# The first mixer's x takes shift and scale in one step, and three context projections and the context's gate products stand ahead of it

## The chip, the cores and the metric

The kernel runs on one core of a Trainium2 chip. The metric is the device time of one execution in microseconds. A run here is such an execution, and the time before is the median of three. One further execution was recorded by the profiler, and all rows below come from that one.

## The reference

The program computes two blocks, one after the other, on 256 tokens of width 1024. The first step, the one that is changed here, is a gated DeltaNet mixer over a latent stream x and a context stream of 256 tokens each:

```
sh1, sc1, ... = split(silu(c) @ ada_w + ada_b, 6)          # for the context: silu(c_ctx)
h  = rms_norm(x) * norm_mix * (1 + sc1) + sh1              # modulate; hl for x, hc for the context
qkv, z, gates, pool_in = split(h @ w_in)
qkv = silu(dw_conv(qkv, conv_w))                           # width 3, along the tokens, zero padded
beta = sigmoid(gates[:2]);  log_decay = -exp(a_log) * softplus(gates[2:] + dt_bias)
o   = gated delta rule over chunks of 64 (k, v of both streams; q of x), forwards and backwards
y   = [rms_norm(o) * silu(z), pooled(pool_in)] @ w_out;    x = x + g1 * y
```

A mixture of 16 experts follows, then a second layer with a short convolution and again 16 experts, and then the second block (an RG-LRU/SSD layer and a stick-breaking layer). None of these is touched by the change.

## The kernel before

**Layout.** Activations lie transposed: 128 features on the partitions, 8 slices of features (`kt`), 256 tokens in a row. Each product runs in three fp32r matmuls per slice, since both weight and activation are split into a high part and a low part (`ws`, lines 344 to 346: high by high, high by low, low by high). The high part is a copy on ScalarE (`wh`, `hl`, `hc`, line 213) and the low part a subtraction on VectorE (`wl`, line 299). `hl` holds x's two parts, `hc` the context's.

**Shift and scale.** The first 8 MB of ada weights (8 tiles) give scale (`ada_first(0)`) and then shift (`ada_first(1)`) of both streams as columns: matmuls at line 482, a copy `adar`, four transposes `adaT`, a reduction and an addition into `adac` (x) and `adax` (context). `norm_in` (line 516) makes `hc` and `hl` from the scale alone. The shift enters later, in two ways. For the projections whose result goes through the convolution, columns 256 and 257 of `hl` hold the two shift columns, so one matmul gives both the projected tokens and the projected shift. The convolution adds the projected shift as a bias, and `edges` (line 691) takes off what that bias must not give at the first and last token (line 555). For the rest, `whole` (unit `U`, line 934) adds the shift to all 8 slices of `hl` and splits them again: on VectorE `lat` and the low part, on ScalarE the high part.

**The hand-written order.** `ORDER["mixer0"]` is a string of units, issued one after another; a scheduler then places the instructions on each engine. kN and vN are the context's projection of head N (`project_ctx`, into `qkvc`); KN, VN and QN are x's projection (`qkv`), with convolution and activation; G is the gates (`qd`: the gate products of x, then of the context; `cum`: sums of the log decays); W0 and W1 are the decay matrices (GpSimd's affine_select and the matmuls `DT`); RN is `correlate` (`kk`), with which a head's matrix A is made; D is `diagonal`, 31 dependent steps on VectorE between L763 and L774; I0 and I1 finish the inverse (`lv`); P0 to P3 run the chunks; Z is the projection of z and of the pooling input (`zp`), which reads the whole `hl`; A0 to A4 are the other ada products, 8 tiles of 1 MB each and 40 in all, at line 439; C0 and C1 are the scores. After the mixer come its output projection (`res`) and the first experts.

**The queue of loads.** SyncE issues all large loads in program order (line 261): the first ada tiles, the mixer's weights (`ev_ws`), the 40 ada tiles through two buffers, `ev_ts`, `ev_out`, and then the experts' `wg`, `wu` and `wd`. A load waits until its buffer is free and holds back all loads behind it.

Of the kernel before, what the change touches and what calls it, by code (L numbers as in the profile page):

```python
# [13 lines left out]
P = 128  # L14
D = 1024
# [8 lines left out]
WARM = 5, 10  # L24
ADA_SUM = ()
# [152 lines left out]
class Kernel:  # L178
# [180 lines left out]
    def quad(self, pool, w32, rhs, n, toks, shift=None):  # L359

        nc = self.nc
        a = self.ps("qd", "a")
        for kt in range(KT):
            q = kt % 4
            r = rhs(kt)
            for i, x in enumerate(r):
                nc.tensor.matmul(a[32 * q:32 * q + 32, :x.shape[1]], w32(kt), x, start=(kt < 4 and i == 0),
                                 stop=(kt >= 4 and i == len(r) - 1), tile_position=(0, 32 * q))  # L370
        s = pool.tile([P, 512], F32, tag="quad", name="quad", bufs=1) if pool else self.work("hid", "quad", 512)
        if shift is None:
            self.copy(s[:, :n], a[:, :n], "act")
        else:
            t, i = shift
            m = t.shape[1]
            if x.shape[1] > n:
                nc.vector.tensor_copy(t, a[:, n:n + m])
            nc.scalar.activation(s[:, :n], a[:, :n], AF.Identity, bias=t[:, i:i + 1])
# [94 lines left out]
    def ada_first(self, i, pool):  # L474
# [12 lines left out]
        for t in range(4):  # L487
            self.tp(b[:, t * P:(t + 1) * P], r[:, t * P:(t + 1) * P])
# [21 lines left out]
    def norm_in(self, pool, wk, hs):  # L510
# [19 lines left out]
        tags = iter(("a", "a", "a", "ps") * 2)  # L530
        for s, f in ((1, s_c), (0, s_l)):
            for ft in range(0, KT, 2):
# [4 lines left out]
                for j in range(2):  # L537
                    self.split_scaled(a[:, 256 * j:256 * j + 256], f[:, ft + j:ft + j + 1],
                                      *(t[:, ft + j, :256] for t in hs[s]))

    def conv3(self, out, a, wc, edges=None):


        for i, x in enumerate(a):
            o = out[:, 256 * i:256 * i + 256]
            if edges is None:
                self.nc.scalar.activation(o, x, AF.Copy, scale=wc[1])
            else:
                self.nc.scalar.activation(o, x, AF.Identity, scale=wc[1], bias=edges[:, i, 2:3])
            self.stt(o[:, 1:], x[:, :255], wc[0], o[:, 1:], OP.mult, OP.add)  # L550
            self.stt(o[:, :255], x[:, 1:], wc[2], o[:, :255], OP.mult, OP.add)
        if edges is not None:
            n = len(a)
            e3 = out[:, :256 * n].rearrange("p (s t) -> p s t", s=n)[:, :, ::255]
            self.nc.vector.tensor_sub(e3, e3, edges[:, :n, :2])
# [12 lines left out]
    def mixer0(self, xin, xp):  # L568
# [20 lines left out]
        self.ada_first(1, xin)  # L589
# [6 lines left out]
        for j, x in enumerate((self.adac[0], self.adax)):  # L596
            self.split(x[:, 0:8], *(t[:, :, 256 + j] for t in hs[0]), "dve")
# [15 lines left out]

        def gates():

            gt = pr.tile([P, 4, 16], F32, name="gates")
            gb = pr.tile([P, 2], F32, name="gate_shift")
            ew = lambda kt: self.col("evgate", 32 * kt, 32)
            for s in range(2):
                gp = self.quad(wk, ew, lambda kt: [t.bitcast(F32) for t in (lat, ctx)[s](kt)], 256, [(0, P), (P, P)], (gb, s))  # L620
# [9 lines left out]
            cum = self.ps("cum", "b")  # L630
# [11 lines left out]
        for dr in range(2):  # L642
            v.tensor_copy(m_out[dr], (self.m_gt, self.m_lt)[dr])

        def decays(dr):
# [3 lines left out]
                                                    base=0, channel_multiplier=-sg)  # L649
            for tt in range(4):  # L650
# [21 lines left out]

        def project_ctx(part, h):

            a = self.ps("qkvc", "b")[:, :256]
            self.ws(a, "ev_ws", 4 * part + h, ctx)
            first[part, h] = a

        def project(part, h):
# [4 lines left out]
            self.ws(a[:, :258], "ev_ws", 4 * part + h, lat)  # L684
# [5 lines left out]
            edges = wk.tile([P, 2, 3], F32, tag="edges", name="edges", bufs=2)  # L690
            v.tensor_mul(edges, a[:, 256:258].unsqueeze(2).to_broadcast([P, 2, 3]), dne[:, i:i + 1].to_broadcast([P, 2, 3]))
# [250 lines left out]
        units = {"G": gates, "W0": each(decays(0), 4), "W1": each(decays(1), 4), "U": whole, "D": invert, "C0": lambda: scores(0), "C1": lambda: scores(1), "Z": each(zpool(), 4)}  # L942
# [69 lines left out]
    def warm(self, n):  # L1012

        x = self.xT.rearrange("p k t -> p (k t)")
        a = self.ps("warm", "ada")
        for i in range(n):
            self.nc.tensor.matmul(a[:, :256], self.ident, x[:, :256], start=True, stop=True)
# [963 lines left out]
```

## Time and profile before

| | us |
|---|---|
| runs | 1247.2, 1247.69, 1238.82 |
| median of the runs | 1247.2 |
| profiled execution, its own time | 1233.16 |
| its span (first to last instruction) | 1231.4 |
| busy: TensorE (PE) / VectorE (DVE) / ScalarE (ACT) / GpSimd (POOL) | 1087.1 / 627.6 / 482.3 / 64.5 |
| first projection of x starts (K0) | 46.44 |
| D starts, on VectorE | 113.82 |
| the inverse starts (`lv`, PE) | 176.18 |
| output projection starts (`res`, PE) | 265.84 |
| first `wd` load issued | 303.95 |

PE is the busiest engine (88% of the span), but the shares are means over stages with different limits; the stages of the mixer are read one by one below. From 320 to 520 us the DMA engines are full (share 1.01, 421 GB/s) while PE is busy for 154.89 of 200 us. A row of the timeline gives its start, its duration, engine, line, operation, result<-inputs and the number of instructions, and in brackets the engine's idle time before it and what ended that. A row of the windows gives the stretch, its length, the busy time of PE, PEld (weight loads into PE), DVE, ACT and POOL with the number of instructions in parentheses, then the granted clock of TensorE (1.00 is the upper level, 2.4 GHz), the busy share of the DMA engines and what they moved in GB/s.

### The profile page before, as it was taken

How to read it: one execution, taken by the hardware profiler on the slowest of the kernel's cores; microseconds unless marked ns; L12 is line 12 of the kernel's file. 1: busy time of each engine (PE TensorE's matmuls, PEld its weight loads, DVE VectorE, ACT ScalarE, POOL GpSimd, SP SyncE). 2: the span in 40 equal slices, each digit the busy share in tenths (PEclk: the TensorE clock that was granted, in tenths of full speed). 3: DMA queues.
4: the chain of work that ended last, by engine and by line, in shares of the span. 5: the costliest groups of instructions: out<-in, count | busy, mean ns of one | idle time of the engine just before them, and what ended most of it. 6: DMA issues, size and time to landing. Idle time of an engine off the chain costs nothing.

```text
span 1231.4 us, 19493 instructions
## 1 busy us (share of the span) xinstructions
PE 1087.1 (88%) x7788; PEld 743.5 (60%) x7788; DVE 627.6 (51%) x1422; ACT 482.3 (39%) x995; POOL 64.5 (5%) x112
## 2 busy tenths in 40 slices
PE   5899889989997666899999766669999999999997
PEld 2667756678443020499863312028897789988875
DVE  3548973363312010478431101028787888689875
ACT  4347543243101000455420100016777566566663
POOL 0050000000000000000000000000001100011100
PEclk9899989989999686999999977789999999999999
DMA  9568567878999999997479999993352145432220
GB/s 384 236 231 305 208 262 240 296 274 367 419 421 420 422 422 422 421 420 290 169 277 421 423 422 420 421 421 111 136 205 82 56 172 189 171 136 106 104 103 35
DMA packets 48042, 339.71 MB, mean 276 GB/s; under 512 B 5328, under 2 KB 5584, under 8 KB 7248
## 3 DMA queue, kind: packets, MB, share of 16 engines
q1 hardware_dynamic: 46800, 336.38, 69.2%
q10 hardware_dynamic: 1152, 2.09, 0.5%
q8 instruction: 61, 1.00, 0.3%
q14 instruction: 29, 0.24, 0.1%
HBM read 337.40 MB, written 1.05 MB: 275 GB/s over the span
## 4 chain that ended last, share of the span: by engine, by line
PE 53%; DMA 27%; DVE 8%; issue 7%; ACT 3%; POOL 2%; POOLq 0%; SPq 0%; DVEq 0%; ACTq 0%
DMA w<-wu 10%; DMA w<-wd 8%; DMA w<-wg 6%; PE ada L439 3%; PE gu L1178 3%; PE sc L346 2%; PE sc L345 2%; PE sc L344 2%; DMA pk<-pk 2%; PE qkvg L344 2%; PE qkvg L346 2%; PE qkvg L345 2%; DVE wl L299 1%; PE res L345 1%; PE res L344 1%
## 5 line engine op out<-in xcount | busy, mean ns | idle before, releaser
L213 ACT ACTIVATE wh<-w 128x512 fp32r<-128x512 f32 x304 | 188.3, 629 | 149.6 <-PE res L345 27.3
L299 DVE TENSOR_TENSOR wl<-w,wh 128x512 fp32r<-128x512 f32 x304 | 208.1, 694 | 74.4 <-ACT wh L213 68.5
L1178 PE MATMUL gu<-w,xg 128*32 128x512 f32 x1024 | 161.0, 734 | 49.6 <-DMA w<-wu 24.8
L1178 PEld LDWEIGHTS gu<-w,xg 128*32 128x32 f32 x1024 | 26.9, 118 | 168.7 <-DMA w<-wu 75.3
L1204 PE MATMUL dn<-w,hidT 128*32 128x512 f32 x512 | 69.3, 638 | 24.9 <-DMA w<-wd 19.1
L1193 DVE TENSOR_TENSOR hid<-hid,gu 128x512 f32<-128x512 f32 x8 | 5.5, 685 | 162.0 <-PE gu L1178 162.0
L213 ACT ACTIVATE y<-dn 128x512 f32<-128x512 f32 x16 | 9.6, 597 | 188.6 <-PE dn L1204 188.6
L234 DVE SCALAR_TENSOR_TENSOR xT<-sc,adac,xT 128x256 f32<-128x256 f32 x64 | 27.9, 479 | 105.4 <-PE sc L1212 105.4
L344 PE MATMUL qkvg<-u_f,wh 128*128 128x272 f32 (+1 forms) x256 | 74.4, 291 | 0.0
L346 PE MATMUL qkvg<-u_f,wl 128*128 128x272 f32 (+1 forms) x256 | 73.2, 286 | 0.0
L345 PE MATMUL qkvg<-u_f,wh 128*128 128x272 f32 (+1 forms) x256 | 72.8, 284 | 0.0
L1204 PEld LDWEIGHTS dn<-w,hidT 128*32 128x32 f32 x512 | 13.9, 113 | 68.9 <-DMA w<-wd 41.1
L346 PE MATMUL sc<-hT,wl 128*128 128x258 f32 x192 | 54.5, 284 | 0.9 <-DVE wl L299 0.9
L344 PE MATMUL sc<-hT,wh 128*128 128x258 f32 x192 | 54.7, 285 | 0.2 <-DVE xT L234 0.2
L345 PE MATMUL sc<-hT,wh 128*128 128x258 f32 x192 | 54.3, 283 | 0.0
L344 PEld LDWEIGHTS qkvg<-u_f,wh 128*128 128x128 f32 x256 | 48.1, 188 | 3.2 <-issue 2.0
L346 PEld LDWEIGHTS qkvg<-u_f,wl 128*128 128x128 f32 x256 | 48.3, 189 | 0.8 <-issue 0.8
L345 PEld LDWEIGHTS qkvg<-u_f,wh 128*128 128x128 f32 x256 | 48.2, 188 | 0.0
L439 PE MATMUL ada<-w,cs 128*32 128x512 f32 x320 | 46.4, 630 | 0.0
L1192 ACT ACTIVATE hid<-gu 128x512 f32<-128x512 f32 x8 | 4.8, 597 | 103.5 <-PE gu L1178 103.5
L1212 PE MATMUL sc<-sg,y 128*128 128x256 f32 x128 | 35.6, 427 | 8.4 <-ACT y L213 8.4
L1212 PEld LDWEIGHTS sc<-sg,y 128*128 128x128 f32 x128 | 25.4, 208 | 25.8 <-ACT y L213 22.5
(606 smaller groups left out, 2620.3 us busy)
## 6 DMA issues: line engine op xcount, KB each, us to landing
w<-wu SPq DMA_DIRECT2D x64, 1024.0 KB, 19.8
w<-wg SPq DMA_DIRECT2D x64, 1024.0 KB, 19.8
w<-wd SPq DMA_DIRECT2D x64, 1024.0 KB, 19.8
w<-ada SPq DMA_DIRECT2D x48, 1024.0 KB, 5.7
w<-f_in SPq DMA_DIRECT2D x16, 1024.0 KB, 4.8
w<-sc_in SPq DMA_DIRECT2D x12, 1024.0 KB, 19.8
w<-e_out SPq DMA_DIRECT2D x8, 1024.0 KB, 4.8
w<-ev_ws SPq DMA_DIRECT2D x6, 1024.0 KB, 5.9
```

Source lines behind the costliest of these rows:

```text
L213: return self.nc.scalar.activation(out, in_, AF.Copy)
L234: return self.nc.vector.scalar_tensor_tensor(out, a, s, b, op0=op0, op1=op1, **kw)
L299: self.nc.vector.tensor_sub(lo, x, hi.bitcast(F32))
L344: mm(out, wh, xh, start=(kt == 0), stop=False)
L345: mm(out, wh, xl, start=False, stop=False)
L346: self.last_mm = mm(out, wl, xh, start=False, stop=(kt == nk - 1)).ins
L439: nc.tensor.matmul(a[32 * q:32 * q + 32, :], self.cs[:, kt, :], w[:, q * 512:(q + 1) * 512], start=(kt == 0), stop=(kt == KT - 1), tile_po ...
L1178: nc.tensor.matmul(a[32 * e:32 * e + 32, :], xg[g // 2][:, kt, s:s + 32], w[:, e * 512:(e + 1) * 512], start=(kt == 0), stop=(kt == KT - 1 ...
L1192: nc.scalar.activation(hid, pu[0], AF.Silu)
L1193: v.tensor_mul(hid, hid, pu[1])
L1204: nc.tensor.matmul(a[32 * e:32 * e + 32, :], hT[:, t, 32 * e:32 * e + 32], w[:, e * 512:(e + 1) * 512], start=(t == 0), stop=(t == 3), til ...
L1212: nc.tensor.matmul(a[:, j * 256:(j + 1) * 256], y[:, (2 * f2 + j) * P:(2 * f2 + j + 1) * P], sg[g // 2][:, g % 2], start=True, stop=True)
```

## The change

x's slices are made after the shift is known, by one step that scales and shifts (`affine`, in turn on ScalarE and VectorE) into `lat`, and are then split. `ada_first(1)` moves into `norm_in`, behind the context's slices. Unit U is gone. Columns 256 and 257 of `hl` now hold the context's shift alone, and the edges are kept for the context's half of K and V only; Q has none and is 256 columns wide. The gate products are a function of their own, `gates_of`: the context's become unit g. Twelve matmuls on constants (`warm`) are added behind the first `adaT`. In the order, k1, k0, g and k2 stand ahead of K0; A tiles, W steps, Q3 and the pieces of Z move as well. Two heads of a context projection share one PSUM bank, and the later context projections and the gate products of the context are held until the shift's last matmul is issued.

```diff
-    "mixer0": "k0 G W1 K0 W1 W0 W0 A0 W1 W0 W1 W0 k1 K1 k2 K2 A1 k3 K3 Q0 R0 R1 R2 R3 v0 V0 v1 V1 v3 V3 v2 V2 Q1 Q2 "
-              "Q3 D A2 I0 I1 A3 I0 I0 I0 U P0 P0 I1 A4 P1 Z I1 I1 C1 C0 P1 Z P2 Z Z P2 P3 P3",
+    "mixer0": "k1 k0 g G k2 K0 W1 W1 W0 A0 W0 W0 W1 W0 K1 K2 A1 k3 W1 K3 Q0 R0 R1 R2 R3 v0 V0 v1 V1 v3 V3 v2 Q3 V2 "
+              "Q1 Q2 D A2 I0 I1 I0 I0 A3 I0 P0 Z P0 I1 A4 Z P1 I1 I1 C1 C0 P1 P2 Z P2 Z P3 P3",
...
+        if i == 0:
+            with self.tc.issue_after(pe.ins):
+                self.warm(WARM0, "b", self.ones)
...
-        for s, f in ((1, s_c), (0, s_l)):
+        for s in (1, 0):
...
+                for k in (ft, ft + 1):
+                    x = a[:, 256 * (k - ft):][:, :256]
+                    if s:
+                        self.split_scaled(x, s_c[:, k:k + 1], *(t[:, k] for t in hs[s]))
+                    else:
+                        t = wk.tile([P, 256], F32, tag="lat", name="lat", bufs=2)
+                        self.affine(t, x, s_l[:, k:k + 1], self.adac[0][:, k:k + 1])
+                        self.split(t, *(t[:, k, :256] for t in hs[s]))
+            if s:
+                self.ada_first(1, pool)
...
-        self.ada_first(1, xin)
+        shift = self.first_mm
...
+        def gates_of(s):
+            with tc.issue_after(shift) if s else ExitStack():
+                qd[s] = self.quad_products(ew, lambda kt: [t.bitcast(F32) for t in (lat, ctx)[s](kt)])
...
         def project_ctx(part, h):
-            a = self.ps("qkvc", "b")[:, :256]
-            self.ws(a, "ev_ws", 4 * part + h, ctx)
+            if (part, h // 2) not in banks:
+                banks[part, h // 2] = self.ps("qkvc", "b")
+            a = banks[part, h // 2][:, 256 * (h % 2):][:, :256]
+            with tc.issue_after(shift) if first else ExitStack():
+                self.ws(a, "ev_ws", 4 * part + h, ctx)
...
-            edges = wk.tile([P, 2, 3], F32, tag="edges", name="edges", bufs=2)
-            v.tensor_mul(edges, a[:, 256:258].unsqueeze(2).to_broadcast([P, 2, 3]), dne[:, i:i + 1].to_broadcast([P, 2, 3]))
+            edges = None
+            if part < 2:
+                edges = wk.tile([P, 3], F32, tag="edges", name="edges", bufs=2)
+                v.tensor_scalar(edges, dne[:, i], a[:, 256:257], None, op0=OP.mult)
...
-        def whole():
-            for ft in range(KT):
-                t = wk.tile([P, 256], F32, tag="sq", name="lat")
-                hi, lo = (t[:, :256] for t in lat(ft))
-                self.stt(t, hi.bitcast(F32), self.adac[0][:, ft:ft + 1], lo.bitcast(F32), OP.add, OP.add)
-                self.split(t, hi, lo)
```

On PE, from the last tiles of the first ada weights to K0, the order before was as follows (`ada` with the waits on DMAHW6 and DMAHW7 are the last two tiles; `qkv` begins K0):

```order
L346 MATMUL qkvc<-hc_292,wl 128x256
L482 MATMUL ada<-w,cs 32x512 [waits DMAHW6_49]
...
L482 MATMUL ada<-w,cs 32x512 [waits DMAHW7_49]
...
L206 MATMUL adaT<-ident,adar 128x128 [waits Activation_49]
...
L369 MATMUL qd<-hl_290,pkg 32x258 [waits DVE_49]
L369 MATMUL qd<-hl_291,pkg 32x258 [waits DVE_49]
...
L344 MATMUL qkv<-hl_290,wh 128x258
```

The same place now:

```order
L486 MATMUL ada<-w,cs 32x512 [waits DMAHW6_49]
...
L486 MATMUL ada<-w,cs 32x512 [waits DMAHW7_49]
...
L207 MATMUL adaT<-ident,adar 128x128 [waits Activation_49]
...
L347 MATMUL qkvc<-hc_305,wl 128x256
L372 MATMUL qd<-hc_305,pkg 32x256
...
L372 MATMUL qd<-hl_303,pkg 32x258 [waits DVE_49,Activation_49]
L372 MATMUL qd<-hl_304,pkg 32x258 [waits DVE_49]
...
L345 MATMUL qkv<-hl_303,wh 128x258
```

The first context projection (k1) now ends ahead of the last two ada tiles; k0, the context's gate products and k2 stand behind them, and x's gate products are spread through k2. Before, only k0 stood ahead, and the context's gate products came after K0 had begun.

On VectorE, in the second half of D, the order before (`sub` and `ident` are D's steps, `wl` a weight's low part, `lat` and `hl` unit U):

```order
L770 TENSOR_TENSOR sub<-B,ident_465 128x112 [waits DVE_49]
L234 SCALAR_TENSOR_TENSOR lat<-hl_290,adac_103,hl_291 128x256 [waits DVE_49]
L771 TENSOR_TENSOR ident_465<-ident_465,sub 128x4x28 [waits DVE_49]
L299 TENSOR_TENSOR wl<-w,wh 128x512 [waits Activation_49]
L770 TENSOR_TENSOR sub<-B,ident_465 128x87 [waits DVE_49]
L299 TENSOR_TENSOR hl_291<-lat,hl_290 128x256 [waits Activation_49]
L771 TENSOR_TENSOR ident_465<-ident_465,sub 128x3x29 [waits DVE_49]
```

The same place now:

```order
L799 TENSOR_TENSOR sub<-B,ident_492 128x112 [waits DVE_49]
L800 TENSOR_TENSOR ident_492<-ident_492,sub 128x4x28 [waits DVE_49]
L799 TENSOR_TENSOR sub<-B,ident_492 128x87 [waits DVE_49]
L800 TENSOR_TENSOR ident_492<-ident_492,sub 128x3x29 [waits DVE_49]
L799 TENSOR_TENSOR sub<-B,ident_492 128x60 [waits DVE_49]
```

The sixteen instructions of U are gone from between D's steps, and the weights' parts stand further ahead.

On SyncE, at the end of the mixer, the loads before:

```order
L261 DMA w<-ada 128x2048 [waits DMAHW7_49,PE_49]
L261 DMA w<-wu 128x2048 [waits DMAHW1_49,PE_49]
L261 DMA w<-wu 128x2048 [waits DMAHW2_49,PE_49]
L261 DMA w<-ev_out 128x2048 [waits DVE_49,Activation_49]
L261 DMA w<-wg 128x2048 [waits DVE_49,PE_49,DMAHW0_49,Activation_49,Pool_49]
```

The same place now:

```order
L262 DMA w<-ada 128x2048 [waits DMAHW7_49,PE_49]
L262 DMA w<-ada 128x2048 [waits DMAHW0_49,PE_49]
L262 DMA w<-ev_out 128x2048 [waits DVE_49]
L262 DMA w<-wg 128x2048 [waits PE_49,DVE_49,Activation_49,Pool_49]
```

Two `wu` loads that were issued ahead of the last `ev_out` loads now come after them, with the other `wu` loads.

## Rows read from the trace of the kernel before

**Rows 1.** Windows of three stages of the mixer; columns as told above.

```profile
60.00:114.00 54.00, 52.61 (x385) 36.93 (x385) 30.66 (x88) 31.86 (x79) 19.50 (x28) 1.00 0.77 270
114.00:176.00 62.00, 55.36 (x357) 39.88 (x355) 56.26 (x152) 31.41 (x71) 0.00 (x0) 0.94 0.67 249
176.00:200.00 24.00, 23.47 (x416) 17.56 (x414) 8.88 (x21) 11.91 (x32) 0.53 (x1) 0.86 0.52 184
```

**Rows 2.** PE's timeline from the end of k0 to the context's gate products.

```profile
35.31 0.28 PE L344 MATMUL qkvc<-hc,wh 128*128 128x256 f32 x1
...
36.63 0.28 PE L346 MATMUL qkvc<-hc,wl 128*128 128x256 f32 x1
36.84 1.92 PE L482 MATMUL ada<-w,cs 128*32 128x512 f32 x16
...
42.61 3.89 PE L369 MATMUL qd<-hl,pkg 128*32 128x258 f32 x32 [2.42 <-DVE hl L214]
46.44 0.58 PE L344 MATMUL qkv<-hl,wh 128*128 128x258 f32 x1
...
48.26 0.28 PE L346 MATMUL qkv<-hl,wl 128*128 128x258 f32 x1
...
48.94 1.97 PE L369 MATMUL qd<-hc,pkg 128*32 128x256 f32 x32
```

**Rows 3.** Window of the two microseconds around the last first-ada loads.

```profile
34.00:36.00 2.00, 2.00 (x17) 1.07 (x16) 1.85 (x4) 0.38 (x1) 0.00 (x0) 1.00 0.07 20
```

**Rows 4.** DVE's timeline: the additions into adac, and weight parts behind them.

```profile
24.08 0.17 DVE L494 TENSOR_TENSOR adac<-adac,pk 128x8 f32<-128x8 f32 x1
...
40.44 1.23 DVE L494 TENSOR_TENSOR adac<-adac,pk 128x8 f32<-128x8 f32 x1
...
42.68 1.89 DVE L299 TENSOR_TENSOR wl<-w,wh 128x512 fp32r<-128x512 f32 x3
```

**Rows 5.** POOL's timeline beside the second addition.

```profile
40.41 1.27 POOL L599 TENSOR_SCALAR_AFFINE_SELECT ident<-ones 128x1024 f32<-128x1024 f32 x1 [26.98 <-DVE adac L493]
```

**Rows 6.** Tile lat: line, operation, count, duration in ns (least/median/most), first and last start.

```profile
L234 DVE SCALAR_TENSOR_TENSOR lat<-hl,adac,hl x8: 475/478/482, 155.6 to 171.9; 128x256 f32<-128x256 f32 x8
L213 ACT ACTIVATE hl<-lat x8: 402/416/420, 156.1 to 172.7; 128x256 fp32r<-128x256 f32 x8
L299 DVE TENSOR_TENSOR hl<-lat,hl x8: 386/418/422, 156.7 to 174.1; 128x256 fp32r<-128x256 f32 x8
```

**Rows 7.** Waits of DVE, 113.8 to 175.7: total, times, longest in us.

```profile
DVE wl L299 <- ACT wh L213: 2.5, 3, 1.8
```

**Rows 8.** SP's timeline: the first experts' loads.

```profile
244.16 3.75 SPq L261 DMA_DIRECT2D w<-wu  x2
...
303.95 2.04 SPq L261 DMA_DIRECT2D w<-wd  x4
```

**Rows 9.** Windows at the head of the experts' stream.

```profile
272.00:276.00 4.00, 4.00 (x31) 3.25 (x31) 2.24 (x4) 1.74 (x4) 0.00 (x0) 1.00 0.03 8
276.00:300.00 24.00, 24.00 (x181) 20.24 (x181) 8.13 (x14) 7.13 (x13) 0.00 (x0) 1.00 1.00 410
300.00:304.00 4.00, 3.90 (x29) 2.90 (x28) 1.06 (x4) 0.69 (x2) 0.00 (x0) 1.00 0.41 168
```

**Rows 10.** PE's timeline: two ada tiles at the mixer's end.

```profile
229.28 1.07 PE L439 MATMUL ada<-w,cs 128*32 128x512 f32 x8
...
232.80 1.07 PE L439 MATMUL ada<-w,cs 128*32 128x512 f32 x8
```

**Rows 11.** Loads issued in 120 to 176: count, size, median us to landing.

```profile
w<-ada SPq DMA_DIRECT2D x9, 1024.0 KB, 7.1
```

**Rows 12.** The same in 176 to 230.

```profile
w<-ada SPq DMA_DIRECT2D x11, 1024.0 KB, 4.9
```

**Rows 13.** POOL's timeline: first and last step of units W0 and W1.

```profile
60.17 0.64 POOL L648 TENSOR_SCALAR_AFFINE_SELECT U<-ld 128x512 fp32r<-128x512 f32 x1 [18.03 <-DVE ld L214]
...
78.00 0.64 POOL L648 TENSOR_SCALAR_AFFINE_SELECT A<-A 128x512 f32<-128x512 f32 x1 [0.67 <-ACT A L656]
```

More of the change, by code (lines that the diff above doesn't have):

```diff
@@ L24 @@
 WARM = 5, 10
+WARM0 = 12
 ADA_SUM = ()
@@ L357, in ts, with quad, quad_products @@
                 mm(out, xl, wh, start=False, stop=(kt == KT - 1))
-    def quad(self, pool, w32, rhs, n, toks, shift=None):
+    def quad(self, pool, w32, rhs, n, toks):
+        return self.quad_sum(pool, self.quad_products(w32, rhs), n, toks)
+    def quad_products(self, w32, rhs):
         nc = self.nc
@@ L370, in quad, with quad_sum @@
                                  stop=(kt >= 4 and i == len(r) - 1), tile_position=(0, 32 * q))
+        return a
+    def quad_sum(self, pool, a, n, toks, shift=None):
+        nc = self.nc
         s = pool.tile([P, 512], F32, tag="quad", name="quad", bufs=1) if pool else self.work("hid", "quad", 512)
@@ L374, in quad @@
         else:
[L375 to L379, printed above, removed]
+            nc.scalar.activation(s[:, :n], a[:, :n], AF.Identity, bias=shift)
         b = self.ps("qd2", "a")
@@ L552, in conv3 @@
         if edges is not None:
-            n = len(a)
-            e3 = out[:, :256 * n].rearrange("p (s t) -> p s t", s=n)[:, :, ::255]
-            self.nc.vector.tensor_sub(e3, e3, edges[:, :n, :2])
+            e3 = out[:, 256:512][:, ::255]
+            self.nc.vector.tensor_sub(e3, e3, edges[:, :2])
     def mixer0_parts(self):
@@ L594, in mixer0 @@
         pp = sub.enter_context(tc.tile_pool(name="m0p", bufs=1))
-        for j, x in enumerate((self.adac[0], self.adax)):
-            self.split(x[:, 0:8], *(t[:, :, 256 + j] for t in hs[0]), "dve")
+        self.split(self.adax[:, 0:8].unsqueeze(2).to_broadcast([P, KT, 2]), *(t[:, :, 256:258] for t in hs[0]), "dve")
         ident32 = pp.tile([P, 32, 32], F32, name="ident32")
@@ L683, in project @@
             a = self.ps("qkv")
-            self.ws(a[:, :258], "ev_ws", 4 * part + h, lat)
+            w = 256 if part == 2 else 258
+            self.ws(a[:, :w], "ev_ws", 4 * part + h, lambda kt: tuple(t[:, :w] for t in lat(kt)))
             segs.insert(0, a[:, :256])
@@ L933, in mixer0 @@
         sw = None
[L934 to L942 removed]
+        units = {"g": lambda: gates_of(1), "G": gates, "W0": each(decays(0), 4), "W1": each(decays(1), 4), "D": invert, "C0": lambda: scores(0), "C1": lambda: scores(1), "Z": each(zpool(), 4)}
         for h in range(4):
@@ L1010, in residual, with warm @@
             yield m
-    def warm(self, n):
-        x = self.xT.rearrange("p k t -> p (k t)")
-        a = self.ps("warm", "ada")
+    def warm(self, n, tag="ada", x=None):
+        x = self.xT[:, 0] if x is None else x
+        a = self.ps("warm", tag)[:, :x.shape[1]]
         for i in range(n):
-            self.nc.tensor.matmul(a[:, :256], self.ident, x[:, :256], start=True, stop=True)
+            self.nc.tensor.matmul(a, self.ident, x, start=True, stop=True)
     def shifted(self, l):
```

31 lines of the change are left out of this document (16 added, 15 removed).

## The prediction

> **What bounds the kernel now.** I read the windows of the mixer first [rows 1], then the timeline of its start on PE, DVE and POOL [rows 2 to 5], then who waits inside D [rows 6, 7], and last the loads behind the mixer [rows 8 to 12]. The stages have different limits. From 60 to 114 us PE is busy for 52.61 of 54 us at full clock: every microsecond of PE work that leaves this stretch brings D's start forward by as much. From 114 to 176 us, the stretch of D, DVE is busy for 56.26 of 62 us, and PE for only 55.36, at a granted clock of 0.94. D's steps depend on each other, so the end of the stretch comes when DVE has done them and all that stands between them. From 176 us PE is the limit again (23.47 of 24 us, clock 0.86). Behind the mixer the experts' loads run at 410 GB/s with a share of 1.00 [rows 9], and their `wd` loads start at 303.95 [rows 8], when the mixer's end has let the buffers go. So whatever the mixer gains or loses, the rest of the program moves with it, about one for one, if the loads ahead of `wd` are through by then.
>
> **The start.** Before K0 begins at 46.44, PE stands still for 2.42 us for the shift columns, and the gate products of x take 3.89 us at the lower clock, where those of the context take 1.97 us later [rows 2]. The last two first-ada tiles ran at 36.84, behind k0. In 34 to 36 us the DMA share was only 0.07, so these tiles had landed by then [rows 3]. In the new order k1 alone stands ahead of them, so they can run at about 35; the gain is 1.9 us, with bounds of 0 (k1 and x's transposes still ahead, as now) and 2.8. What follows them, to the end of the addition into `adac` at 40.44 + 1.23 = 41.67 [rows 4], is the same chain, so x's shift is there at about 39.8. Then x is made: on ScalarE 4 `affine` steps and 8 high parts, on VectorE 4 and 8 low parts. There is no such `affine` in the trace; I take it as a copy or an addition of the same shape, 0.42 to 0.48 us [rows 6]. That is 12 x 0.42 = 5.0 on ScalarE and 4 x 0.48 + 8 x 0.42 = 5.3 on VectorE, plus three weight parts of 1.89 us in all that stand there too [rows 4]: 7.2 us. K0 follows at 39.8 + 7.2 = 47.0, 0.6 us **later** than now (bounds: 1 us earlier if the weight parts slip behind, 3 us later if the two engines wait for each other at every slice).
>
> What PE does meanwhile is what counts. A context projection is 24 matmuls; twelve of them start over 36.63 - 35.31 = 1.32 us, 0.12 us apart [rows 2], so one is 2.9 us. Two of them (k1, k2) and the context's gate products (1.97) stand ahead of K0 that stood behind it: 2 x 2.88 + 1.97 = **7.7 us** less PE work between K0 and D. They fill the time in which PE waited, so they cost nothing as long as x's path takes those 7 us; if x were ready at once, they would delay it by as much. With PE at work, K0 should also begin at full clock: its first nine matmuls start over 48.26 - 46.44 = 1.82 us instead of 8 x 0.12 = 0.96 [rows 2], **0.9 us**. The twelve `warm` matmuls run while PE has nothing else, between the first `adaT` and k1, and I cost them at nothing; if the first slices of the context came earlier, they would cost their own 12 x 0.12 = 1.4 us. D's start moves forward by 7.7 + 0.9 - 0.6 = **8.0 us**.
>
> At one place the trace and the Trainium skill meet. The addition into `adac` took 1.23 us at 40.44, against 0.17 us for the same one at 24.08 [rows 4]; from 40.41 to 41.68 POOL made `ident` [rows 5], which is released by the reduction just before. The chain of the new kernel has the same addition at its head, beside the same POOL instruction, so by the rows the sum does not change. The Trainium skill, "SBUF — State Buffer", section "Who interferes with whom", says that a DVE instruction with two SBUF inputs contends with a GpSimd instruction that reads SBUF. The low parts of x have two such inputs, so by that rule, if `ident` slid from the addition to them, up to another 1.1 us would go, and the gain below would be 13.2 us.
>
> **The stretch of D.** U's 8 `lat` (0.478) and 8 low parts (0.418) leave VectorE: 7.2 us as busy time [rows 6]. Back to back, instructions start a little before the last has ended, so I take 6.0, with bounds of 5.5 and 7.2. Their cover was nothing: they stand between D's steps. U also delayed Z's projections, which read the new `hl`, and with them the next weights: DVE waited 1.8 us once for a `wh` whose buffer Z's matmuls still held, 2.5 us in all [rows 7]. With U gone I count 1.5 of it (0 to 2.5). Q's edges and their corrections go, one accumulation of Z comes into the stretch; I set these against each other as nothing. Together **7.5 us**, between 5.5 and 9.7. PE has room for this: 62 - 55.36 = 6.6 us idle and (1 - 0.94) x 55.4 = 3.3 us of clock, 9.9 in all [rows 1]. By the order three of the 40 ada tiles, 3 x 1.07 = 3.2 us [rows 10], move from ahead of the last `kk` to behind it. D starts earlier by that, but PE has to do them in a stretch that is then nearly full, so I count nothing.
>
> **The loads.** Two `wu` loads that were issued at 244.16 [rows 8], in the mixer, now stand behind the last `ev_out`, among the others. At 410 GB/s 1.05 MB takes 2.56 us [rows 9], so 5.1 us of loading come later. From 272 to 276 us the engines were idle but for a share of 0.03, 3.9 us in which they can be done. That leaves **1.2 us** lost (bounds 0, since from 300 to 304 another 2.4 us were idle, and 5.1).
>
> **The sum.** 8.0 + 7.5 - 1.2 = 14.3 us. Against the profiled execution's 1233.16 that is 1218.9; the median of the runs, 1247.2, stands 14.0 above it, so the forecast is 1247.2 - 14.3 = **1233**. One per cent, 12.5 us, is about what a measurement of this kernel can tell from no change, so this is only just a gain.
>
> **The rivals.**
> 1. *D does not start earlier.* The gates come from x's products, and these are not earlier than now. From them follow the W steps on POOL, in a row from 60.17 to 78.64 [rows 13], 19.5 us of POOL in the stretch [rows 1], and each head's A needs them. If PE then waits where it worked, the 8.0 us go and 1247.2 - 7.5 + 1.2 = 1241 is left. For it: POOL is nearly without gaps there. Against it: D starts 35 us after W's end, and PE, not POOL, was full in between.
> 2. *PE full throughout.* The three tiles do bring D forward, and PE, without its waits, is granted the full clock: 8.0 + 9.9, and in 176 to 200 another (1 - 0.86) x 23.5 = 3.3 us [rows 1], less 1.2, is 20.0, 1227. Against it: the trace has idle time at every change of stage.
> 3. *The loads eat it.* Both `wu` loads count in full, 5.1 instead of 1.2: 1237.
> 4. *Slower: the ada tiles.* They go through two buffers, and the order now has 19 of them behind the start of `lv` instead of 16, up to the output projection, at the spacing of the end of the mixer, 3.5 us [rows 10]. Two tiles take a load and a use, so the spacing is at least half of landing + 1.07; at the measured landing of 4.9 [rows 12] there is up to 1.0 of slack. Landing took 7.1 in 120 to 176 [rows 11]; with the whole mixer in less time, it may there too. From 7 us on this decides: the spacing becomes 4.0 to 4.5, 19 x 0.75 = 14 us, all of the gain. At 8.5 the spacing is 4.8 to 5.3, 19 x 1.55 = 29 us are lost, and 1233 + 29 = 1262. Against it: the loads that slow those in 120 to 176 (`ev_ts`) are not there later.
>
> **Chances.** Forecast 0.42, rival 1 0.23, rival 2 0.15, rival 3 0.10, rival 4 0.10. Faster by over 1% are rival 2, some six tenths of the forecast's case and a little of rival 3: 0.44. Slower by over 1% is most of rival 4: 0.08. The rest, 0.48, lies within 1%. The range reaches from rival 2 to rival 1; the terms' bounds and the runs, which lie 9 us apart, add some 5 or 6 us on each side: 1222 to 1247.
>
> **What would show it.** K0's first `qkv` at about 47, with two `qkvc` projections and the context's `qd` ahead of it, and its matmuls 0.12 us apart. L792, D's first transpose, at about 106 instead of 113.82. From there to the first `lv` about 55 us instead of 62, with no `lat` in it, and DVE still the fuller engine; if PE is full there, rival 2 or its limit decides. `res` at about 250 instead of 265.84. DMA share near 1 from `wg` on, without the hole of 272 to 276. I am wrong if K0 starts after 50, if PE shows waits for `DT` or U tiles between 60 and 100, or if ada tiles follow each other at more than 4 us behind `lv` with PE waiting for them.

## The result, and the profile after

The changed kernel took 1226.33 us (median of 4 runs, 1223.81 to 1231.17), the kernel before, on the same chip, 1243.01 (4 runs). The ratio on record is 0.9893, with a 95% interval of 0.9849 to 0.9937: 1.07% faster, about 13 us. It is not the quotient of these two medians, which are 16.7 us apart. A second set of runs of the changed kernel gave a median of 1226.29 against 1240.48 for 23 runs of the kernel before, 14.2 us, and a ratio of 0.9881 [0.9832, 0.9929]. The forecast was 14.3 us less, to 1233. The difference was met; 1233 itself is 7 us too high, since it starts from a median of three runs, 1247.2, and the longer sets of the kernel before have medians of 1239.0 to 1241.4.

One profiled execution of each does not show this: 1233.16 us before, 1228.43 after, 4.7 us apart. A second execution of each (1237.86 before, 1219.37 after) is 18.5 us apart. So the stages are compared one by one, over both pairs:

| start of, us | before, two traces | changed, two traces | moved by |
|---|---|---|---|
| K0 (PE) | 46.4, 47.0 | 51.4, 50.4 | +3.4 to +5.0 |
| D (VectorE) | 113.8, 114.6 | 107.3, 106.5 | -6.5 to -8.1 |
| the inverse, `lv` (PE) | 176.2, 176.8 | 164.3, 163.4 | -11.9 to -13.4 |
| output projection (PE) | 265.8, 266.5 | 260.1, 247.5 | -5.7 to -19.0 |
| router of the second experts, last `lg` (PE) | 620.1, 621.1 | 614.5, 603.2 | -5.6 to -17.9 |

The first three lines repeat within a microsecond. The fourth does not, and there the two executions of the changed kernel part. These are the windows from K0 to D, from D to `lv`, the 30 us behind `lv`, and from there to the output projection; the columns are those of [rows 1]. Before:

```profile
46.44:113.82 67.38, 65.99 (x502) 47.43 (x500) 38.00 (x118) 36.23 (x88) 19.50 (x28) 0.99 0.70 247
113.82:176.18 62.36, 55.72 (x359) 40.07 (x358) 56.57 (x154) 31.76 (x72) 0.00 (x0) 0.95 0.67 249
176.18:206.18 30.00, 29.47 (x488) 22.58 (x488) 12.15 (x31) 11.75 (x31) 0.53 (x1) 0.89 0.58 198
206.18:265.84 59.66, 56.39 (x420) 40.62 (x419) 29.25 (x86) 21.05 (x57) 2.01 (x2) 0.95 0.84 298
```

The changed kernel, first execution, and the two stretches of loads that answer to [rows 9]:

```profile
51.41:107.34 55.93, 53.50 (x389) 38.29 (x388) 37.70 (x116) 35.01 (x88) 19.85 (x28) 1.00 0.69 246
107.34:164.30 56.96, 55.27 (x376) 41.41 (x374) 52.17 (x132) 29.35 (x66) 0.00 (x0) 1.00 0.77 291
164.30:194.30 30.00, 30.00 (x398) 22.94 (x399) 8.31 (x21) 8.87 (x23) 0.53 (x1) 0.54 0.43 150
194.30:260.10 65.80, 62.89 (x524) 43.79 (x522) 32.74 (x94) 22.64 (x64) 2.02 (x2) 1.00 0.83 291
272.00:276.00 4.00, 4.00 (x31) 3.24 (x30) 1.70 (x4) 1.56 (x3) 0.00 (x0) 1.00 1.02 428
300.00:304.00 4.00, 3.99 (x20) 3.54 (x21) 3.33 (x12) 1.75 (x4) 0.00 (x0) 1.00 1.01 422
```

The changed kernel, second execution:

```profile
50.40:106.50 56.10, 53.68 (x390) 38.27 (x389) 37.62 (x116) 34.91 (x88) 19.80 (x28) 1.00 0.69 245
106.50:163.40 56.90, 55.21 (x377) 41.37 (x375) 52.16 (x132) 29.32 (x66) 0.00 (x0) 1.00 0.77 291
163.40:193.40 30.00, 30.00 (x515) 23.44 (x516) 12.67 (x33) 13.06 (x37) 0.52 (x1) 1.00 0.60 214
193.40:247.50 54.10, 51.23 (x406) 35.12 (x404) 28.31 (x82) 18.44 (x48) 2.01 (x2) 1.00 0.90 319
```

Read the third row of each. It is the same program, and PE is busy all the time, but at a granted clock of 0.54 it gets through 398 matmuls, at 1.00 through 515. From `lv` to the output projection one execution takes 95.8 us and the other 84.1. PE runs 919 matmuls and stands still for 2.9 us in both, so the 11.7 us between them go with the clock alone:

```profile
164.30:260.10 95.80, 92.89 (x919) 66.73 (x919) 41.05 (x115) 31.52 (x86) 2.54 (x3) 0.86 0.70 247
163.40:247.50 84.10, 81.23 (x919) 58.55 (x919) 40.98 (x115) 31.51 (x85) 2.54 (x3) 1.00 0.79 282
```

Before, both executions had 0.89 in the 30 us behind `lv`. K0 to D is 11.4 us shorter (67.38 to 55.93), D to `lv` 5.4 (62.36 to 56.96), and in D's stretch PE is now the fuller engine (55.27 of 56.96 us; VectorE 52.17). The hole in the loads at 272 us is gone: the share is 1.02. D's first step and the first `lv` of the first execution:

```profile
107.34 0.70 DVE L792 STREAM_TRANSPOSE Ac<-Ad 128x512 f32<-128x512 f32 x1
164.30 0.59 PE L824 MATMUL lv<-RT,A 32*32 32x32 f32 x13 [0.39 <-DVE RT L803]
```

At the start, the changed kernel's PE from the context's gate products to K0 (answers to [rows 2]):

```profile
40.04 1.97 PE L372 MATMUL qd<-hc,pkg 128*32 128x256 f32 x32
...
46.73 0.62 PE L372 MATMUL qd<-hl,pkg 128*32 128x258 f32 x2
47.28 0.39 PE L345 MATMUL qkvc<-hc,wh 128*128 128x256 f32 x1
47.51 0.28 PE L346 MATMUL qkvc<-hc,wh 128*128 128x256 f32 x1
47.62 0.28 PE L347 MATMUL qkvc<-hc,wl 128*128 128x256 f32 x1
47.83 0.62 PE L372 MATMUL qd<-hl,pkg 128*32 128x258 f32 x2
48.38 0.38 PE L345 MATMUL qkvc<-hc,wh 128*128 128x256 f32 x1
...
51.41 0.28 PE L345 MATMUL qkv<-hl,wh 128*128 128x258 f32 x1
```

And its VectorE and GpSimd around the shift and the end of x's path (answers to [rows 4, 5]):

```profile
38.25 0.17 DVE L502 TENSOR_TENSOR adac<-adac,pk 128x8 f32<-128x8 f32 x1
...
45.59 0.41 DVE L300 TENSOR_TENSOR hl<-lat,hl 128x256 fp32r<-128x256 f32 x1
45.92 1.77 DVE L670 CAST m_out<-m_lt 128x128 fp32r<-128x128 f32 x1
47.13 0.63 DVE L670 CAST m_out<-m_gt 128x128 fp32r<-128x128 f32 x1
47.68 0.41 DVE L300 TENSOR_TENSOR hl<-lat,hl 128x256 fp32r<-128x256 f32 x1
```

```profile
45.88 1.27 POOL L612 TENSOR_SCALAR_AFFINE_SELECT ident<-ones 128x1024 f32<-128x1024 f32 x1 [32.69 <-DVE lat L223]
```

The shift is there at 38.4 instead of 41.7. x's last low part waits behind a cast that took 1.77 us beside GpSimd's mask, and ends at 48.1; K0 begins 3.3 us after that.

### The profile page after: what moved, and what is told of

It is laid out like the page before. It is cut to its first block, busy times and chain, and to the rows that moved or that the text cites. A ratio compares the mean times of both kernels' runs of the same rounds, so it can differ in the third digit from the quotient of the medians.

```text
span 1226.7 us, 19522 instructions
## 1 busy us (share of the span) xinstructions
PE 1089.6 (89%) x7812; PEld 748.3 (61%) x7812; DVE 624.7 (51%) x1400; ACT 480.3 (39%) x991; POOL 65.5 (5%) x112
## 4 chain that ended last, share of the span: by engine, by line
PE 39%; DMA 24%; issue 7%; DVE 5%; ACT 2%; POOL 1%; POOLq 0%; DVEq 0%; SPq 0%; ACTq 0%
DMA w<-wd 10%; DMA w<-wg 6%; DMA w<-wu 6%; PE gu L1199 4%; PE sc L347 2%; PE sc L346 2%; PE sc L345 2%; PE qkvg L345 2%; PE xg L1174 2%; PE qkvg L347 2%; PE qkvg L346 2%; DMA pk<-pk 1%; PE dn L1225 1%; PE res L346 1%; PE res L345 1%
## 5 line engine op out<-in xcount | busy, mean ns | idle before, releaser
L1199 PE MATMUL gu<-w,xg 128*32 128x512 f32 x1024 | 155.6, 714 | 49.5 <-DMA w<-wu 27.4
L1199 PEld LDWEIGHTS gu<-w,xg 128*32 128x32 f32 x1024 | 27.2, 117 | 163.4 <-DMA w<-wu 75.2
L1225 PEld LDWEIGHTS dn<-w,hidT 128*32 128x32 f32 x512 | 13.5, 114 | 71.2 <-DMA w<-wd 46.4
L345 PEld LDWEIGHTS qkvg<-u_f,wh 128*128 128x128 f32 x256 | 48.1, 188 | 3.2 <-issue 2.0
L1233 PE MATMUL sc<-sg,y 128*128 128x256 f32 x128 | 40.2, 469 | 9.1 <-ACT y L214 9.1
L1233 PEld LDWEIGHTS sc<-sg,y 128*128 128x128 f32 x128 | 28.2, 231 | 28.6 <-ACT y L214 24.2
L1213 ACT ACTIVATE hid<-gu 128x512 f32<-128x512 f32 x8 | 4.8, 598 | 100.7 <-PE gu L1199 100.7
```

Source lines behind the costliest of these rows:

```text
L345: mm(out, wh, xh, start=(kt == 0), stop=False)
L1199: nc.tensor.matmul(a[32 * e:32 * e + 32, :], xg[g // 2][:, kt, s:s + 32], w[:, e * 512:(e + 1) * 512], start=(kt == 0), stop=(kt == KT - 1 ...
L1225: nc.tensor.matmul(a[32 * e:32 * e + 32, :], hT[:, t, 32 * e:32 * e + 32], w[:, e * 512:(e + 1) * 512], start=(t == 0), stop=(t == 3), til ...
L1233: nc.tensor.matmul(a[:, j * 256:(j + 1) * 256], y[:, (2 * f2 + j) * P:(2 * f2 + j + 1) * P], sg[g // 2][:, g % 2], start=True, stop=True)
```

## The experiments

All were timed against the kernel before on the same chip, on one of two chips; the ratio on record, with its 95% interval, is to those runs, and can differ a little from the quotient of the medians. The changed kernel itself stands at 0.9893 and 0.9881.

**The changed kernel again.** No edit.

> The changed kernel as it is, a second execution with its trace. Theory A (the gain ahead of the inverse is 12 us and half of it is lost to a low TensorE clock behind it): first lv at 164 +- 1, granted clock in the 30 us behind it again 0.5 to 0.6, output projection at 259 to 261, time 1.0 to 1.4% below the kernel before. Rival B (the low clock was chance of one execution): clock there 0.8 or more, output projection at about 250, and such an execution some 10 us shorter.

Measured: 1226.29 us, ratio 0.9881 [0.9832, 0.9929]; the trace is the second one above. `lv` at 163.4 as expected; the clock behind it was 1.00, not 0.5 to 0.6, and the output projection at 247.5. Of Theory A its first half holds (12 us are gained ahead of `lv`); for this low clock being of one execution, Rival B is right. Its size, 11.7 us, is that of the forecast's whole gain.

**The kernel before again.** No edit.

> The kernel before as it is, a second execution with its trace. The first one (1233.16 us) was shorter than all its timed runs. If the low clock behind lv is what its executions differ by: first lv again at 175 to 177, granted clock in the 30 us behind it 0.5 to 0.7 instead of 0.88, output projection 5 to 10 us later than 265.84, time 1238 to 1246. If they differ elsewhere: output projection at 265 to 267.

Measured: 1237.86 us, output projection at 266.5, and again 0.89 behind `lv`:

```profile
176.80:206.80 30.00, 29.45 (x488) 22.58 (x488) 12.11 (x31) 11.75 (x31) 0.52 (x1) 0.89 0.58 197
```

So it is not this stretch in which these two executions of the kernel before differ: at 621.1, the last `lg`, they are 1.0 us apart, and the other 3.7 us come behind the experts. My guess that the dip explains the spread of its runs is not borne out by these two executions; what the spread comes from is open.

**Full-array matmuls between the inverse's groups.**

```diff
             for p, A, Yi, YT, R, C, r, c in blocks:
                 for t, h in th:
-                    mm(a[q4(c), 0, t, h], ...
+                    last = mm(a[q4(c), 0, t, h], ...
+            with tc.issue_after(last.ins):
+                self.warm(LVWARM, "a", self.ones)     # LVWARM = 4; the same behind the next group
```

> The changed kernel with four full-array matmuls on constants (128x128, 0.22 us each) added after each of the first two groups of each inverse, 16 in all, 3.5 us of PE at full clock and more at the lower one. Theory A: they keep the granted clock up in the 30 us behind the first lv (0.54 in the changed kernel), worth up to 10 us, so the output projection starts 3 to 7 us earlier. Rival (the clock of that stretch is not set by what PE runs there, or its PE time is hidden): the clock stays at 0.5 to 0.6, and the program is 3 to 7 us longer for the added work.

> The changed kernel with two instead of four full-array matmuls behind each of the four groups, 8 in all, 1.8 us. If two hold the clock as well: 1.5 to 3 us below lv_warm, 1222 to 1224, mean clock of the runs 0.942 or more. If not: the clock of most runs is 0.938 or less, 1226 to 1232.

> The kernel before with the same 16 full-array matmuls on constants in the inverse that held the clock up in the changed kernel (lv_warm, 1225.5 us). With the clock held in both, the pair tells the change's own part. Theory A (the change gains 12 us ahead of lv and some behind it, whatever the clock does): 1236 to 1240, so 11 to 14 us above lv_warm. Rival B (the change's gain is partly the clock of its executions): 5 us or less above lv_warm.

Measured: 1225.51 (0.9894 [0.9857, 0.993]) with four, 1225.14 (0.9888 [0.9848, 0.9929]) with two, and 1239.54 (0.9989 [0.9967, 1.0011]) for the kernel before with four. The 30 us behind `lv`, of the changed kernel with four and with two, and of the kernel before with four:

```profile
164.30:194.30 30.00, 29.99 (x508) 23.69 (x512) 10.54 (x25) 10.91 (x30) 0.52 (x1) 1.00 0.62 221
```

```profile
165.10:195.10 30.00, 29.93 (x502) 23.64 (x503) 12.21 (x32) 10.90 (x30) 0.52 (x1) 1.00 0.53 183
```

```profile
178.20:208.20 30.00, 30.00 (x511) 23.35 (x511) 10.31 (x24) 11.77 (x32) 0.52 (x1) 1.00 0.66 230
```

The clock was 1.00 in all three traces; of the eleven traces without these matmuls, one has 1.00 there. But the output projection came at 255.4 and 254.7, not at 247.5, and the median of the changed kernel does not move. With two matmuls `lv` to the output projection takes 89.6 us at full clock, 5.5 more than in the second execution of the changed kernel; the added work is 1.8 of it, and the rest I can't place.

On one chip the changed kernel with two and the kernel before with four are 14.4 us apart (1225.14 and 1239.54). With four in both it is 14.0, but these two ran on different chips; by their ratios it is about 12. That is more than the 5 us of Rival B in the last of these expectations, so a gain that is only the clock of the executions is out. It is not a clean measure of the change's own part, though. The kernel before, then the changed kernel, with four, from `lv` to the output projection:

```profile
178.20:274.20 96.00, 87.34 (x938) 66.33 (x937) 41.50 (x115) 33.28 (x89) 2.54 (x3) 0.97 0.70 247
164.30:255.40 91.10, 87.60 (x951) 63.36 (x951) 41.16 (x115) 31.69 (x86) 2.54 (x3) 0.98 0.80 284
```

In the kernel before PE stood still for 8.7 us here, 3.4 of them for one load (`poolm`), and the output projection came at 274.2, 8 us later than without the added matmuls. This execution, 1245.49 us, was the longest of its twelve.

**Z's pieces held back behind the first group of the inverse.**

```diff
-                self.ts(aa, lat, "ev_ts", part, range(0, 4))
+                with tc.issue_after(self.lv_mm) if part else ExitStack():
+                    self.ts(aa, lat, "ev_ts", part, range(0, 4))
                 yield
-                self.ts(aa, lat, "ev_ts", part, range(4, 8))
+                with tc.issue_after(self.lv_mm):
+                    self.ts(aa, lat, "ev_ts", part, range(4, 8))
```

> The changed kernel, but the last three of Z's four pieces are issued on PE only behind the first lv group: 24 zp matmuls stand ahead of lv instead of 61. Theory A: the stretch of D then has 8.6 us less PE work and is set by VectorE again (52 us busy), so first lv comes 4 to 5 us earlier, at 159 to 160, and full-array zp matmuls stand between the lv groups, so the clock there is 0.7 or more; output projection 3 to 8 us earlier than the changed kernel's. Rival (PE work is only moved, and the clock falls all the same): lv earlier, output projection at 259 to 262 as before.

Measured: 1238.82, ratio 0.9978 [0.9954, 1.0002]: all of the gain gone. From D to the first `lv`, and the 30 us behind it:

```profile
106.50:161.10 54.60, 46.21 (x339) 34.78 (x337) 50.42 (x128) 25.61 (x59) 0.00 (x0) 0.97 0.77 288
161.10:191.10 30.00, 29.96 (x388) 21.23 (x389) 4.37 (x15) 8.35 (x22) 0.52 (x1) 0.50 0.37 120
```

D's stretch is 2.4 us shorter, less than expected; PE stands still for 8 us in it, of which it waits 6.3 us for the last transpose (RT), and then gets a clock of 0.50:

```profile
161.14 0.90 PE L824 MATMUL lv<-RT,A 32*32 32x32 f32 x13 [6.30 <-DVE RT L803]
```

The held pieces did not land between the groups, as was expected: in the 30 us behind `lv` PE runs 4 of Z's matmuls, where the changed kernel has 6, and 68 only later. So this run does not tell whether full-array work there would have held the clock. It does tell that 9 us of PE work taken out of D's stretch shorten it by only 2.4.

**The old string of units on the changed kernel.**

```diff
-    "mixer0": "k1 k0 g G k2 K0 W1 W1 W0 ...
+    "mixer0": "k0 g G W1 K0 W1 W0 W0 A0 W1 W0 W1 W0 k1 K1 k2 K2 A1 k3 K3 Q0 ...   # the string before, without U
```

> The changed kernel with the string of units as it was before, without U and with g right ahead of G: one context projection ahead of x instead of three. If the 7.7 us of PE work moved ahead of K0 is a real gain: K0 starts at 45 to 47, PE waits there for x, D starts 4 to 6 us later than in the changed kernel, and the program is 3 to 6 us longer than that. If the order brings nothing and U's removal all of it: within 2 us of the changed kernel.

Measured: 1241.58, ratio 1.0014 [0.999, 1.0037]. D starts at 113.5, as before; D to `lv` takes 59.0 us; behind it the clock is 0.61, PE waits 4.1 us for ada tiles, and the output projection is at 272.5:

```profile
113.50:172.50 59.00, 57.10 (x375) 41.95 (x375) 54.10 (x136) 30.33 (x67) 0.00 (x0) 1.00 0.71 264
172.50:202.50 30.00, 28.65 (x395) 21.31 (x395) 5.72 (x17) 8.16 (x21) 0.52 (x1) 0.61 0.41 143
```

So x's new path alone, without the order, brings nothing. The loss is larger than the 3 to 6 us that were expected, since the stretch behind `lv` goes wrong too.

**U taken out of the kernel before.**

```diff
-              "Q3 D A2 I0 I1 A3 I0 I0 I0 U P0 P0 I1 ...
+              "Q3 D A2 I0 I1 A3 I0 I0 I0 P0 P0 I1 ...
```

> The kernel before without U: x's slices never get their shift for Z, so z and the pooling input are those of x without it. This prices U in the kernel before, with the wait of Z. Forecast's term: D to lv is 7.5 us shorter (62.4 to about 55), between 5.5 and 9.7, and the output projection as much earlier at equal clock. Rival B (PE takes over as the limit at once): 3 to 4 us shorter, as with the old string of units in the changed kernel (59.0).

Measured: 1238.13, ratio 0.9984 [0.9959, 1.0009]. D to `lv` takes 60.2 us, only 2.2 less, less than either theory had. VectorE's groups in that stretch tell why; in the kernel before 21 low parts of weights and none of Z's accumulations stand there, and without U:

```profile
L299 DVE TENSOR_TENSOR wl<-w,wh 128x512 fp32r<-128x512 f32 x24 | 16.4, 685 | 1.5 <-ACT wh L213 1.4
...
L234 DVE SCALAR_TENSOR_TENSOR zp<-zp 128x512 f32<-128x512 f32 x2 | 1.4, 678 | 0.0
```

Three low parts and two accumulations, 3.4 us, moved into the holes that U left. With the 5.7 us that U costs when it is put back (next run), 5.7 - 3.4 = 2.3 remain, about what was measured. Behind `lv` the clock is 0.60 instead of 0.89, and the output projection is at 268.7, later than before:

```profile
174.30:204.30 30.00, 30.00 (x405) 23.51 (x406) 5.72 (x17) 9.36 (x25) 0.52 (x1) 0.60 0.38 139
```

**U's work put back into the changed kernel.**

```diff
+        def dummy_u():
+            for ft in range(KT):
+                t = wk.tile([P, 256], F32, tag="sq", name="ulat")
+                hi, lo = (t[:, :256] for t in lat(ft))
+                self.stt(t, hi.bitcast(F32), self.adac[0][:, ft:ft + 1], lo.bitcast(F32), OP.add, OP.add)
+                self.split(t, *(wk.tile([P, 256], F32R, tag=n, name=n) for n in ("uh", "ul")))
-... A3 I0 P0 Z P0 ...
+... A3 I0 U P0 Z P0 ...
```

> The changed kernel with U's sixteen VectorE and eight ScalarE instructions put back ahead of P0, into tiles that nobody reads (x already has its shift). This prices U's engine time alone, without the wait of Z for it. Theory A (PE is the limit of D's stretch now: 55.3 of 57.0 us, VectorE 52.2): of the 7.2 us on VectorE 4 to 5 are hidden, so D to lv takes 59 to 60 us instead of 57 and the program is 2 to 3 us longer. Rival B (D's chain on VectorE still sets the stretch): 63 to 64 us, program 6 to 7 us longer.

Measured: 1239.72, ratio 0.998 [0.9948, 1.0012]. D to `lv` takes 62.6 us, 5.7 more than in the changed kernel:

```profile
106.60:169.20 62.60, 57.19 (x385) 40.83 (x383) 57.93 (x152) 33.52 (x78) 0.00 (x0) 0.96 0.79 293
169.20:199.20 30.00, 30.00 (x391) 23.05 (x391) 6.72 (x17) 7.51 (x18) 0.52 (x1) 0.51 0.34 125
```

Most of U's 7.2 us counts; Rival B is nearer than Theory A. VectorE is busy for 5.8 us more than in the changed kernel and idle as long as there (4.7 and 4.8 us). The output projection of the profiled execution is 7.3 us later than in the first execution of the changed kernel, the median 13. The twelve runs part by the granted clock of the whole program: three with 0.938 took 1227 to 1232 us, the other nine, with 0.923 to 0.933, 1237 to 1243. So most of these 13 us go with a lower clock; why it is low in nine of twelve is open.

**x's gate products in one block; and the mask for D issued later.**

```diff
-    "mixer0": "k1 k0 g G k2 K0 ...
+    "mixer0": "k1 k0 g k2 G K0 ...
-            with tc.issue_after(shift) if s else ExitStack():
+            with tc.issue_after(shift if s else self.last_mm):      # x's products behind k2, K0 behind those
...
+        with tc.issue_after(x_lo):                                  # second kernel only
+            g.affine_select(ident32, ...
```

> The changed kernel with x's 16 gate products in one block behind k2 (in the changed kernel they stand in nine places within k2) and K0 behind them. Theory A: the late K0 (51.4 instead of 47) comes from PE's switches between 32-column gate products and full-array projections, 0.4 to 0.5 us each, not from x's path, which ends at 47.7: K0 starts at 47.5 to 48.5, D 2.5 to 3.5 us earlier than in the changed kernel (at 103.5 to 105). Rival B: x's path sets K0, and the products only fill the wait: K0 at 50 to 51, D unchanged.

> As the run before it, and GpSimd's mask for D (ident, 1.27 us) is issued only behind x's last low part. In the changed kernel a cast on VectorE took 1.77 us beside it, ahead of that low part. Theory A (the two engines hold each other up there): the cast takes 0.2 us or is behind, x's last low part starts 1 to 1.4 us earlier (at 45.2 to 46.6 instead of 46.6 to 47.7), and K0 by about 1 us. Rival B (the cast's time is its own): x's last low part unchanged within 0.3 us.

Measured: 1232.17 (0.9943 [0.9908, 0.9977]) and 1231.2 (0.9917 [0.9884, 0.9949]). In the first kernel, PE ahead of K0:

```profile
44.95 1.97 PE L372 MATMUL qd<-hl,pkg 128*32 128x258 f32 x30
47.81 0.62 PE L372 MATMUL qd<-hl,pkg 128*32 128x258 f32 x2 [0.90 <-DVE hl L300]
48.37 0.39 PE L345 MATMUL qkv<-hl,wh 128*128 128x258 f32 x1
```

K0 starts at 48.4, as Theory A has it: the switches cost the changed kernel 2 to 3 us there. But D starts only 0.7 to 1.5 us earlier: from K0 to D PE stands still for 3.5 us of 57.4, where it was 2.4 of 55.9; 1.5 of it is for GpSimd's tiles (0.9 in the changed kernel). The first `lv` is at 161.2, 2 to 3 us earlier. From there to the output projection it then takes 100.7 us, longer than in either trace of the changed kernel, and the clock behind `lv` is low again, 0.60 (0.57 in the second kernel):

```profile
161.20:191.20 30.00, 29.96 (x407) 22.03 (x408) 8.83 (x22) 10.48 (x27) 0.52 (x1) 0.60 0.38 129
```

The low clock can be part of this, but not all of it, since 0.54 went with 95.8 us. The intervals of both kernels overlap that of the changed kernel, so that they are slower is likely and not shown; why, is not settled. In the second kernel the mask still ran at 45.93, beside the cast, which took 1.31 us: the edit did not move it, and the question it was to answer is not answered by it.

**No matmuls on constants at the start.**

```diff
-WARM0 = 12
+WARM0 = 0
```

> The changed kernel without the twelve matmuls on constants behind the first adaT. The prediction costs them at nothing and counts 0.9 us for K0 at full clock. If the work ahead of K0 keeps the clock by itself: K0 and D within 0.5 us of the changed kernel's, same time. If k1 then runs at the lower clock: 22 to 47 us at a clock of 0.9 or less, K0 and D 1 to 2 us later.

Measured: 1226.68, ratio 0.9901 [0.9865, 0.9938]. From 22 us to K0:

```profile
22.00:52.50 30.50, 27.23 (x201) 16.03 (x194) 16.10 (x46) 13.33 (x31) 1.81 (x2) 0.94 0.64 266
```

The clock is 0.94 instead of 1.00, K0 at 52.5 and D at 108.4, 1.1 us later than in one trace of the changed kernel and 1.9 in the other, as expected; in the time of the whole no difference can be seen.

## Why the prediction was right, and where its terms were off

The mechanism was right: D comes earlier by the PE work moved ahead of it, D's stretch is shorter by U, and the rest of the program follows. The sum, 14.3 us, is borne out by the ratios (13 to 15 us) and fits the kernels with added matmuls (12 to 14, though these are no clean measure). That it comes so near is in part luck: errors of several us in its terms cancel, and the clock behind `lv`, which it did not foresee, moves single executions by as much. The terms, one by one:

- **D's start, forecast 8.0 us earlier.** Measured 6.5 to 8.1. Errors cancel. *K0 was to start 0.6 us later; it starts 3.4 to 5.0 later.* The mis-sized step is the one that let PE's work ahead of x cost nothing. The shift was there at 38.4 instead of the forecast 39.8: the last two tiles ran 2.2 us earlier (1.9 was forecast) and the addition took 1.1 us less. x's path from there took 9.7 us instead of 7.2, to 48.1 instead of 47.0. That alone would have put K0 about 1 us behind the forecast. But x's 16 gate products were spread over seven places, one ahead of k2 and six within it (the expectation of that run says nine), and an island of one product, 0.12 us of work, takes 0.55 us before a projection's matmul follows (47.83 to 48.38). Put in one block, K0 follows the last product at 48.4. On the other side I counted the *three ada tiles* that moved out of the way of D as nothing, because PE would have to do them in D's stretch. They are not there: nine tiles stand in D's stretch in both traces, 12 instead of 15 between K0 and D, and 19 instead of 16 behind `lv`. So they shortened K0 to D by their 3.2 us. The forecast's own K0 to D, 7.7 + 0.9 = 8.6 us shorter, plus 3.2 is 11.8; measured 11.4.
- **D's stretch, forecast 7.5 us shorter.** Measured 5.4, below the lower bound of 5.5. U was to give 6.0 and the waits 1.5; VectorE's busy time fell by 4.4 (56.57 to 52.17) and its idle time by 1.0. Put back, U's instructions count 5.7 of their 7.2, near the 6.0. Why 4.4 and not 5.7 left the stretch is not shown: in the kernel before without U, 3.4 us of low parts and accumulations of later projections moved up, but in the changed kernel there are 20 low parts in it instead of 21, and one accumulation, which the forecast had. PE is nearly full there now (55.27 of 56.96 us), as the prediction's limit had it, with 15 more of Z's matmuls and 13 more of the context's projections. By the two runs that vary it, VectorE still sets most of the length: 5.8 us more of its work cost 5.7, and 9 us less of PE's (with 1.8 us less of VectorE's) gave 2.4.
- **Loads, forecast 1.2 us lost.** From the first `lg` to the second experts' it takes 318.2 us before, 319.6 and 321.1 after: 1.2 to 2.9 us lost. The hole of 272 us is filled (share 0.03 then, 1.02 now).
- **The addition beside GpSimd, and the Trainium skill's rule** ("SBUF — State Buffer", "Who interferes with whom"). The addition now takes 0.17 us; GpSimd's mask slid to the end of x's path, as the rule's case had it, but what stood beside it there was a cast of 128x128, not a low part. It took 1.77 us. In the kernel before, the same cast stood behind GpSimd's mask:

```profile
42.15 0.16 DVE L643 CAST m_out<-m_lt 128x128 fp32r<-128x128 f32 x1
```

  The section also names casts among the DVE instructions that can take the ports shared with GpSimd. The traces fit that: the cast ends within 0.1 us of the end of a GpSimd instruction, at 47.69 beside a memset that follows the mask and ends at 47.62, and in the run with x's products in one block at 47.20, beside the mask's end at 47.11. No run took the mask away, so the cause is argued from these times. By my estimate about 1.2 us of x's path went there (1.1 had been the price): the last low part started 1.6 us after its high part was done (46.12 to 47.68), and two casts of 0.16 us stand between. It did not show in the total, as K0 then waited for k2 and its switches.
- **Rivals.** *D not earlier*: wrong, PE waited 0.9 us for GpSimd's tiles between K0 and D. *PE full throughout, 1227*: PE is full, and in one execution it had the clock too; that one took 1219.37, 13.8 below the first execution of before, where this rival had 20.0. That its 1227 is nearer to the measured 1226 than the forecast's 1233 is owed to the starting median of 1247.2. *The loads eat it*: no. *Slower, by ada tiles*: PE waited 0.5 us for them behind `lv`. In the old order it waited 4.1 us there, so that price is real in other orders.
- **What no case had: the clock behind the inverse.** 0.89 before; 0.54 and 1.00 in two executions of the changed kernel, worth 11.7 us. The forecast took [rows 1], 0.86, as it stood.

**The order and U's removal need each other.** The new path of x with the old order: 1.0014. U out of the kernel before: 0.9984. The order with U's work still in it: 0.998. Both: 0.9893 and 0.9881. Each alone gives earlier marks that are spent before the output projection, partly on the clock behind `lv` (0.61, 0.60 and 0.51 in these three). Why the stretch has 0.89 in the kernel before, and 0.54 or 1.00 in the changed one, is open; with full-array matmuls between the groups it was 1.00 in three traces of three, and the medians did not move. No version here is shown to be faster than the changed kernel.

## What to carry to other kernels

Price a moved step by the stage's limiting engine, and then look at what else in the program order can slip into the hole: here 3.4 of the 7.2 us that U's removal freed on VectorE were taken by later work. When filler work is interleaved with short matmuls of another tile shape, count the switches, not only the matmuls. Where a stage of small matmuls stands on the path, compare two executions before believing a difference between two profiles: the granted clock of that one stage can outweigh the change.

## What the runs showed of the hardware that I had not expected

- The granted clock of one stretch of the same program was 0.54 in one execution and 1.00 in another: 398 against 515 matmuls in 30 us. Ahead of the fall PE had run 32x32 matmuls for 2.2 us; in the execution without a fall it had run the same ones. Ten matmuls of the same shape, of the inverse's first group, ahead of the fall and behind it:

```profile
165.64 0.48 PE L824 MATMUL lv<-R,A 32*32 32x32 f32 x10
...
166.95 0.72 PE L824 MATMUL lv<-RT,A 32*32 32x32 f32 x10
```

- An island of one gate product (128x32 tiles; two matmuls in the trace) between full-array projections takes 0.55 us from its start to the next matmul's, where in a block one product takes 0.12 (1.97 us for 16 of them). The Trainium skill ("TensorEngine Tiling (Array Packing)", section "Key Properties") says that changing the tiling mode drains TensorE, and gives no price; the trace fits that, with 0.55 against 0.12 us.
- The cast beside GpSimd's mask: 1.77 us in two executions of the changed kernel, 1.31 in two other kernels, 0.16 behind the mask.
